# Gated DeltaNet on Trainium2: the recurrence from pair 2 on placed one slot later among the dense products

## The chip, the core and the metric

The kernel runs on one core of a Trainium2 chip. The metric is the device time of one execution in microseconds. A core has four compute engines that run their own instruction streams and meet by semaphores: TensorE (PE in the profile, with its weight loads as PEld), VectorE (DVE), ScalarE (ACT) and GpSimd (POOL). SyncE (SP) issues the DMAs of this program.

## What is computed

One inference step of a trunk of two layers over a prompt of 1024 tokens with 16 meta tokens ahead of it, and a batch of eight samples of eight tokens each. Layer 0 is a gated DeltaNet, layer 1 an RWKV-7 layer. The change concerns layer 0 alone. With `xn` the normed input, it computes (cut from the reference):

```python
proj = xn @ w_in                                     # q, k, v, z and two gates per head
qkv, new_buf = causal_conv(qkv, conv_buf, conv_w)    # 4 taps, then silu
q, k = l2norm(q) * GDN_HEAD_K ** -0.5, l2norm(k)
L = strict_lower((beta * k) @ k.T * decay)           # per chunk of 64 tokens
u, wk = solve(I + L, [beta * v, beta * k * exp(gc)])
for each chunk:                                      # the recurrence, S is [key, value]
    v_new = u - wk @ S
    o     = (q * exp(gc)) @ S + attn @ v_new
    S     = S * exp(g_last) + k_dec.T @ v_new
o = rmsnorm(o, gn_w) * silu(z)
return o @ w_out, S, new_buf
```

There are 8 key heads and 16 value heads of 128, so 8 head pairs, each one key head with its two value heads.

## The kernel before

**Tiling.** The tokens stand in three segments of 384, 384 and 336 columns (SEGS), nine token groups of 128 in all. A dense product (`product`, `halves`) is 128 output features over all tokens in split precision: per segment 24 matmuls of 128x128 by 384 or 336 columns, in two halves of 12. The 12 matmuls of a half are one *slot*. A product has six slots, two for each segment; the last two of six are the narrow ones of 336 columns.

**Order of the products.** `ORDER` (L26) lists the products by pair: k, q, and v, w (the two value heads), x, y (the gates z of the pair before); the last pair has its own gates X, Y as well. 48 products make 288 slots, numbered from −24 to 263. From pair 1 on a pair takes six products, 36 slots: pair 1's begin at slot 0, pair 2's at 36, pair 7's at 216. I call the stretch of 36 slots a period, and count its slots from 0 to 35.

**What is placed among them.** `gdn_events` (L923) fills a table of events, each with a time in slots, and a loop in `layer0` (its function `before`) emits, behind the 12 matmuls of a slot, all events whose time lies below the next slot. On TensorE and ScalarE the instructions run in just this order (`manual_schedule`). VectorE, GpSimd and SyncE are ordered by the scheduler of the framework, from the same program. Two groups of events are made for each pair j:

- `chain_events(j, G, a)` with a = first[j]: the recurrence (`gdn_recur`, 9 token groups, three steps each, a step per slot) and what goes with it: the decays and scores of attention, the token transposes (ktok), the sample states, the norm of the outputs and the gated transposes (`gdn_norm_out`, tile mog).
- `front_events(j, G, b, a, a0)` with a0 = first[j − 1]: the preparation of pair j's triangular solve while pair j − 1's recurrence runs: decays E, scores, blocks, 15 calls of the inverse (`inverse32`, L573 and L575 on VectorE), `spread` at a − 9.9 (copy invA at L743, store to DRAM as g_t and g_u, load back as T1n at L749 and TT at L756), and four merges at a − 6.5, a − 4.5, a − 3.5 and a − 1.5. The first merge issues the 72 small matmuls rY, which read T1n and E.

A token group of the recurrence reads on TensorE: S,K and S,Q (state by keys and by queries); then X,TT, where X is made on VectorE (L883); then w,ktok and w,attn, where w is scaled on ScalarE. VectorE closes the group with the new S (L905) and the output o (L916). The next group's S,K needs this S, and its PSUM tile the rA of an earlier group to be read.

The times of pair 2's `front_events` hang on first[1], those of later pairs on first[j − 1]. Not tied to first are the products, the conv taps and silus behind them (`vt`, `cvy`, `raw`), the sample keys, the weight casts (`whi`, `wlo`) and their loads (`wraw`). Weights are loaded two tiles of 256 KB at a time into two buffers, and a buffer is free when `wlo` was made from it on GpSimd. Behind slot 263 follow the rest of pair 7's recurrence, the reload of the gated outputs (`load_split`), the residual (`residual_in`) and the output projection (`gdn_out`).

Of the kernel before, what the change touches and what calls it, by code (L numbers as in the profile page):

```python
# [36 lines left out]
class Builder:  # L37
# [885 lines left out]
    def gdn_events(self, G, open_, gate, swap):  # L923

        self.events = {}
        base = [-24]
        for j in range(8):
            base.append(base[j] + 6 * min(len(ORDER[j]), 6))
        first = [9, 43] + [base[j + 1] + 6 for j in range(2, 8)]
        for u in (-23.4, -21.4, -20.4):  # L930
            self.at(u, gate)
        self.at(-13, swap)
        for j in range(8):
            self.chain_events(j, G, first[j])
            self.front_events(j, G, base[j] if j else -24, first[j], first[j - 1] if j else None, open_)
# [1618 lines left out]
```

## Time and profile before

| | us |
|---|---|
| median of 3 runs | 2171.39 |
| lowest and highest | 2170.72, 2176.32 |
| the profiled execution | 2173.21 |
| its span, first to last instruction | 2171.5 |
| mean granted TensorE clock | 0.982 |
| the stretch read below, slots 36 to 263 of layer 0's products (about) | 247 to 1015 |
| a steady period (36 slots), of which TensorE is busy | 118.80, 116.99 |

The page of the profile gives the busy time of each engine, the chain of work that ended last, and the costliest groups of instructions. A row of the timeline gives start, length, engine, line of the kernel, operation, output and inputs without buffer numbers, shape, count, and in brackets the idle time of the engine just before it with the instruction that ended it. A row of waits gives engine, waiting line, what it waited for, total us, times and the longest. In rows of windows stand the start and end, the length, busy us and count for PE, PEld, DVE, ACT and POOL, then the granted clock, the share of the DMA engines and GB/s.

### The profile page before, as it was taken

What the parts mean: (1) busy time and instruction counts of PE and PEld (TensorE: products, weight loads), DVE (VectorE), ACT (ScalarE), POOL (GpSimd) and SP (SyncE); (2) the same over time, 40 slices, a digit from 0 to 9 for tenths busy, and PEclk for the clock granted to TensorE, in tenths of its full rate; (3) what the DMA queues carried; (4) which work ended last, traced back from release to release, by engine and by line L of the source; (5) the groups of instructions that cost most, each with busy time, mean ns of one, the idle gap of its engine ahead of it and who ended that gap; (6) DMA issues with size and microseconds to landing.
All of it is one profiled execution on the core that took longest, in us unless ns stands there. A gap on an engine that the chain in (4) does not pass through costs nothing. (4 is left out here: it accounts for less than half of the span.)

```text
span 2171.5 us, 54811 instructions
## 1 busy us (share of the span) xinstructions
PE 2046.2 (94%) x20418; PEld 1905.8 (88%) x20418; DVE 1583.4 (73%) x4212; ACT 1283.1 (59%) x3750; POOL 834.9 (38%) x1136
## 2 busy tenths in 40 slices
PE   6969899999999999999999999889899999999997
PEld 5959899999999999998899999889798988888876
DVE  6968879698888979795334676757979557767755
ACT  4536565656565665656533365664747446677774
POOL 3523334334343333334231352344524254444444
PEclk9979999999999999999999999999999999999999
DMA  3424343424333333335345115655555486677754
GB/s 120 122 58 105 77 108 90 118 79 107 90 97 106 106 97 104 97 102 159 106 129 135 63 54 191 220 160 174 169 180 158 117 224 175 188 234 225 228 178 139
DMA packets 430724, 292.52 MB, mean 135 GB/s; under 512 B 147337, under 2 KB 413050, under 8 KB 430458
## 3 DMA queue, kind: packets, MB, share of 16 engines
q1 hardware_dynamic: 430458, 289.02, 46.2%
q8 instruction: 161, 2.64, 0.5%
q14 instruction: 105, 0.86, 0.1%
HBM read 197.55 MB, written 91.37 MB: 133 GB/s over the span
## 5 line engine op out<-in xcount | busy, mean ns | idle before, releaser
L91 POOL TENSOR_TENSOR wlo<-wraw,whi 128x512 fp32r<-128x512 f32 (+1 forms) x246 | 331.1, 1348 | 465.6 <-ACT whi L87 413.9
L77 PE MATMUL d<-xc,whi 128*128 128x384 f32 (+2 forms) x1006 | 279.5, 337 | 4.8 <-ACT whi L87 4.1
L526 DVE SCALAR_TENSOR_TENSOR cvy<-raw,cw,cvy 128x408 f32<-128x408 f32 (+2 forms) x288 | 199.0, 692 | 17.1 <-ACT cvy L63 15.7
L87 ACT CAST whi<-wraw 128x512 fp32r<-128x512 f32 (+1 forms) x246 | 149.8, 611 | 88.1 <-PE d L77 51.2
L77 PEld LDWEIGHTS d<-xc,whi 128*128 128x128 f32 (+1 forms) x1006 | 183.4, 189 | 7.8 <-ACT whi L87 4.8
L77 PE MATMUL d<-xc,wlo 128*128 128x384 f32 (+3 forms) x476 | 157.7, 340 | 2.7 <-POOL wlo L91 2.7
L77 PE MATMUL dz<-xc,whi 128*128 128x384 f32 (+1 forms) x480 | 153.9, 338 | 0.0
L77 PE MATMUL dv<-xc,whi 128*128 128x384 f32 (+1 forms) x480 | 152.4, 337 | 0.0
L77 PE MATMUL d<-xa,whi 128*128 128x384 f32 (+3 forms) x450 | 142.1, 340 | 4.5 <-ACT whi L87 1.7
L63 ACT ACTIVATE o<-rA,gcol 128x128 f32<-128x128 f32 x128 | 42.0, 366 | 116.9 <-DVE S L905 116.7
L573 DVE TENSOR_TENSOR invtmp<-invA,invT 72x31 f32<-72x31 f32 (+15 forms) x248 | 102.2, 412 | 3.2
L77 PE MATMUL dv<-xa,whi 128*128 128x384 f32 (+1 forms) x288 | 99.1, 344 | 0.0
L77 PE MATMUL dz<-xa,whi 128*128 128x384 f32 (+1 forms) x288 | 98.6, 342 | 0.0
L575 DVE TENSOR_TENSOR invT<-invT,invtmp 72x31 f32<-72x31 f32 (+15 forms) x248 | 95.0, 383 | 3.3
L77 PEld LDWEIGHTS d<-xc,wlo 128*128 128x128 f32 (+1 forms) x476 | 89.3, 189 | 6.8 <-POOL wlo L91 3.6
L77 PEld LDWEIGHTS dz<-xc,whi 128*128 128x128 f32 x480 | 89.4, 189 | 4.6 <-issue 4.5
L77 PEld LDWEIGHTS d<-xa,whi 128*128 128x128 f32 (+1 forms) x450 | 83.9, 189 | 8.2 <-issue 3.7
L77 PEld LDWEIGHTS dv<-xc,whi 128*128 128x128 f32 x480 | 89.2, 188 | 1.4 <-issue 1.4
L77 PE MATMUL d<-xa,wlo 128*128 128x384 f32 (+3 forms) x252 | 84.9, 337 | 1.4 <-POOL wlo L91 1.4
L77 PE MATMUL dk<-xc,whi 128*128 128x384 f32 (+1 forms) x240 | 79.3, 349 | 0.0
L77 PE MATMUL dq<-xc,whi 128*128 128x384 f32 (+1 forms) x240 | 77.0, 338 | 0.0
L1335 DVE SCALAR_TENSOR_TENSOR mixs<-xb,pcol,mixs 128x320 f32<-128x320 f32 (+2 forms) x96 | 68.6, 725 | 5.9 <-ACT mixs L63 5.6
(542 smaller groups left out, 6801.0 us busy)
## 6 DMA issues: line engine op xcount, KB each, us to landing
wraw<-in_gdn_w_in SPq DMA_DIRECT2D x96, 256.0 KB
wraw<-in_rwkv_w_rkvz SPq DMA_DIRECT2D x80, 256.0 KB
Sb<-in_state_gdn SPq DMA_DIRECT2D x64, 256.0 KB
sldcak<-cakd SPq DMA_DIRECT2D x24, 576.0 KB
wraw<-in_rwkv_w_o SPq DMA_DIRECT2D x42, 256.0 KB
E<-drow SPq DMA_DIRECT2D x24, 384.0 KB
attn<-drow SPq DMA_DIRECT2D x24, 384.0 KB
wraw<-in_gdn_w_out SPq DMA_DIRECT2D x36, 256.0 KB
```

Source lines behind the costliest of these rows:

```text
L63: return self.nc.scalar.activation(out, in_, func, bias=bias, scale=scale, **kw)
L77: self.nc.tensor.matmul(out, lhsT, rhs, start=start, stop=stop)
L87: nc.scalar.copy(hi, x)
L91: e.tensor_tensor(lo, x, hi.bitcast(F32), op=ALU.subtract)
L526: nc.vector.scalar_tensor_tensor(y[0][:, 0:wd], raw[:, k:k + wd], cw[k], y[0][:, 0:wd], op0=ALU.mult, op1=ALU.add)
L573: nc.vector.tensor_tensor(tmp, A[:, j, j + 1:32].unsqueeze(2).broadcast_to([nb, n, m]), Tv[:, j, 0:m].unsqueeze(1).broadcast_to([nb, n, m] ...
L575: nc.vector.tensor_tensor(Tv[:, j + 1:32, 0:m], Tv[:, j + 1:32, 0:m], tmp, op=ALU.subtract)
L1335: nc.vector.scalar_tensor_tensor(x[:, f:], xb[:, 8 + a + f:8 + b], mu, x[:, f:], op0=ALU.mult, op1=ALU.add)
```

## The change

One number in the table of starts: for the pairs from 2 on, the recurrence starts at the base of the next period plus 7 instead of plus 6. Pairs 0 and 1 keep their starts 9 and 43 (43 is 36 + 7).

```diff
         base = [-24]
         for j in range(8):
             base.append(base[j] + 6 * min(len(ORDER[j]), 6))
-        first = [9, 43] + [base[j + 1] + 6 for j in range(2, 8)]
+        first = [9, 43] + [base[j + 1] + 7 for j in range(2, 8)]
```

So all of `chain_events` for pairs 2 to 7 comes one slot later, the merges of pairs 2 to 7 too, and the decays, scores, inverse and spread of pairs 3 to 7. Every engine has the same instructions as before; only their order differs, and in layer 1 TensorE's order is the same.

The first place is TensorE in slot 29 and 30 of the period in which pair 5's recurrence runs (S_10372 and S_10398 are its state, dv a product of pair 6, f the transposes of values, mog the gated transposes). Before, behind the 12 matmuls of slot 29, which has 336 columns:

```order
L77 MATMUL rA_11455<-S_10372,K_8774 128x128
L77 MATMUL rA_11456<-S_10372,K_8774 128x128
L77 MATMUL rA_11455<-S_10372,Q_9575 128x128
L77 MATMUL rA_11456<-S_10372,Q_9575 128x128
L74 MATMUL f_11468<-ident_74,vt_11376 128x128 x3
L74 MATMUL mog_11478<-ident_74,o_10797 128x128
L74 MATMUL mog_11478<-ident_74,o_10909 128x128
L74 MATMUL mog_11478<-ident_74,o_11029 128x128
```

Now, in slot 30, which has 384 columns:

```order
L77 MATMUL rA_11490<-S_10398,K_8731 128x128
L77 MATMUL rA_11491<-S_10398,K_8731 128x128
L77 MATMUL rA_11490<-S_10398,Q_9552 128x128
L77 MATMUL rA_11491<-S_10398,Q_9552 128x128
L74 MATMUL mog_11507<-ident_74,o_10816 128x128
L74 MATMUL mog_11507<-ident_74,o_10929 128x128
L74 MATMUL mog_11507<-ident_74,o_11046 128x128
```

The last token group's S,K stands behind a wide slot now instead of a narrow one, and so do those of the groups that stood in slots 11, 17 and 23.

The second place is TensorE at the end of a period, slots 35 and 0, with the twelve products of a slot between them left out. Before:

```order
L74 MATMUL f_11719<-ident_74,vt_11667 128x128 x3
L77 MATMUL rY_11729<-T1n_510,E_10262 32x32 x12
L77 MATMUL rY_11730<-T1n_510,E_10354 32x32 x12
L77 MATMUL rY_11731<-T1n_510,E_10433 32x32 x12
```

and behind the next slot:

```order
L74 MATMUL mog_11807<-ident_74,o_11156 128x128
L74 MATMUL mog_11807<-ident_74,o_11318 128x128
L74 MATMUL mog_11807<-ident_74,o_11450 128x128
L74 MATMUL flast_11813<-ident_74,last_10059 108x128
```

Now the f transposes stand alone in slot 35, and behind slot 0 stand these:

```order
L77 MATMUL rY_11760<-T1n_510,E_10285 32x32 x12
L77 MATMUL rY_11761<-T1n_510,E_10372 32x32 x12
L77 MATMUL rY_11762<-T1n_510,E_10448 32x32 x12
L74 MATMUL flast_11805<-ident_74,last_10012 108x128
```

The small products rY, which read T1n, come behind slot 0 instead of slot 35, and the first three mog have gone to slot 1.

The third place is what leads to T1n of pair 6, on VectorE and on SyncE (invT_10716 and invT_10733 are the inverse, bv is made from the f transposes, ovar belongs to the norm). VectorE before:

```order
L905 SCALAR_TENSOR_TENSOR S_10372<-S_10372,eglb_136,rA_11456 128x128
L575 TENSOR_TENSOR invT_10716<-invT_10716,invtmp_11532 72x2x30
L825 TENSOR_TENSOR bv_11560<-f_11561,sk_10081 128x3x128
L573 TENSOR_TENSOR invtmp_11591<-invA_10714,invT_10716 72x31
L916 TENSOR_TENSOR o_11450<-o_11450,rA_11455 128x128
L916 TENSOR_TENSOR o_11450<-o_11450,rA_11456 128x128
L575 TENSOR_TENSOR invT_10716<-invT_10716,invtmp_11591 72x31
L526 SCALAR_TENSOR_TENSOR cvy_11567<-raw_11498,cw_404,cvy_11567 128x408
L743 COPY invA_10714<-invT_10716 72x1024
```

VectorE now:

```order
L905 SCALAR_TENSOR_TENSOR S_10398<-S_10398,eglb_136,rA_11491 128x128
L526 SCALAR_TENSOR_TENSOR cvy_11544<-raw_11469,cw_404,cvy_11544 128x408
L575 TENSOR_TENSOR invT_10733<-invT_10733,invtmp_11555 72x3x29
L916 TENSOR_TENSOR o_11485<-o_11485,rA_11490 128x128
L916 TENSOR_TENSOR o_11485<-o_11485,rA_11491 128x128
L573 TENSOR_TENSOR invtmp_11558<-invA_10731,invT_10733 72x60
L575 TENSOR_TENSOR invT_10733<-invT_10733,invtmp_11558 72x2x30
L573 TENSOR_TENSOR invtmp_11608<-invA_10731,invT_10733 72x31
L825 TENSOR_TENSOR bv_11643<-f_11644,sk_10034 128x3x128
L575 TENSOR_TENSOR invT_10733<-invT_10733,invtmp_11608 72x31
L1059 SCALAR_TENSOR_TENSOR ovar_11635<-ssq_11184,qeps_9537 128x6
L743 COPY invA_10731<-invT_10733 72x1024
```

Before, the bv ahead of the last step reads the f transposes of slot 31; now it reads those of slot 33. From the inverse's first step to the copy invA, VectorE has 140 rows instead of 136: two taps (cvy), one vt, one bv and one ovar more, one zg less. SyncE before:

```order
L920 DMA out_p_gdn<-S_10372 128x2x128
L746 DMA g_t<-invT_10716 54x1024
L745 DMA g_u<-invA_10714 72x1024
L749 DMA T1n_510<-g_t 32x18x32 x3
L756 DMA TT_13_117<-g_u 32x6x32 x4
L756 DMA TT_14_118<-g_u 32x6x32 x4
L756 DMA TT_11_115<-g_u 32x6x32 x4
L428 DMA wraw_11778<-in_gdn_w_in 128x4x128
L428 DMA wraw_11780<-in_gdn_w_in 128x4x128
```

SyncE now:

```order
L920 DMA out_p_gdn<-S_10398 128x2x128
L428 DMA wraw_11731<-in_gdn_w_in 128x4x128
L746 DMA g_t<-invT_10733 54x1024
L745 DMA g_u<-invA_10731 72x1024
L749 DMA T1n_510<-g_t 32x18x32 x3
L756 DMA TT_13_117<-g_u 32x6x32 x4
L756 DMA TT_14_118<-g_u 32x6x32 x4
L756 DMA TT_11_115<-g_u 32x6x32 x4
L428 DMA wraw_11733<-in_gdn_w_in 128x4x128
```

One of the two wraw loads stands ahead of g_t now, in all of pairs 3 to 7; for pair 2 the order of these rows is unchanged.

## Prediction

> **What bounds the kernel now.** I read the page first (parts 1 and 4), then windows over the eight pair periods of the DeltaNet layer, the waits of TensorE inside them, and the timeline at the slots that those waits name. The page:
>
> ```profile
> span 2171.5 us, 54811 instructions
> ...
> PE 2046.2 (94%) x20418; PEld 1905.8 (88%) x20418; DVE 1583.4 (73%) x4212; ACT 1283.1 (59%) x3750; POOL 834.9 (38%) x1136
> ```
>
> TensorE is busy for 94% of the span. Only the DeltaNet layer is touched, so the share has to be read there. The windows cut it by pair period (the 36 slots of six products; columns: window, length, busy us and count of PE, PEld, DVE, ACT, POOL, granted clock, DMA share, GB/s). The first row is a whole steady period, the next two lie inside it, the last is the tail behind the products:
>
> ```profile
> 734.30:853.10 118.80, 116.99 (x1027) 111.09 (x1021) 102.00 (x280) 74.17 (x246) 43.37 (x66) 1.00 0.36 100
> ...
> 831.00:842.00 11.00, 9.95 (x69) 9.47 (x68) 10.92 (x31) 5.17 (x18) 1.85 (x5) 1.00 0.32 91
> 842.00:853.10 11.10, 11.10 (x138) 10.54 (x137) 11.00 (x31) 4.73 (x14) 5.81 (x9) 1.00 0.58 146
> ...
> 1015.00:1060.00 45.00, 38.86 (x269) 35.48 (x268) 19.86 (x50) 34.61 (x153) 13.07 (x13) 1.00 0.60 182
> ```
>
> A steady period leaves TensorE 118.80 − 116.99 = 1.8 us idle, so a later recurrence can win little per period. VectorE is the second engine, and in the last 22 us of a period it is full (10.92 of 11.00, 11.00 of 11.10 us): what is put ahead of something there delays it. TensorE's waits in the five periods from pair 2's recurrence on (376.5 to 972.5; engine, line, waited for: us, times, longest):
>
> ```profile
> PE rA L77 <- DVE o L916: 4.2, 7, 0.7
> PE mog L74 <- ACT o L63: 2.4, 4, 0.6
> PE rA L77 <- DVE S L905: 1.5, 5, 0.3
> ```
>
> So 5.7 us are the recurrence's S,K products waiting for VectorE, and 2.4 us the gated output's transposes waiting for ScalarE. Where they stand in a period (start, length, instruction, idle before and its releaser):
>
> ```profile
> 832.93 0.32 PE L77 MATMUL dv<-xc,wlo 128*128 128x336 f32 x1
> 833.09 0.32 PE L77 MATMUL dv<-xc,whi 128*128 128x336 f32 x1
> 833.71 0.49 PE L77 MATMUL rA<-S,K 128*128 128x128 f32 x2 [0.31 <-DVE S L905]
> 834.95 0.49 PE L77 MATMUL rA<-S,K 128*128 128x128 f32 x2 [0.74 <-DVE o L916]
> ...
> 856.40 0.33 PE L74 MATMUL mog<-ident,o 128*128 128x128 f32 x1 [0.59 <-ACT o L63]
> ```
>
> The first two waits are in slot 29 of the period, a slot of 336 columns, which covers the chain least; the third is in slot 0 of the next. A stall costs more than its bracket: from the last dv to the S,K it waits for lie 833.71 − 833.09 = 0.62 us, where matmuls of that width follow each other 0.16 us apart (832.93 to 833.09), so 0.46 is lost for 0.31 listed. I take 1.5 times the listed idle throughout.
>
> **The change, part by part.** No instruction is added or removed; every cost is one of place.
>
> *Pair 2's T1n.* In before, the inverse's small products rY at the end of slot 71 wait for the DMA of T1n, and then the clock drops (the last rows are the same place a few pairs later, at full clock, a whole slot of dk matmuls from 853.10 to 855.31):
>
> ```profile
> 374.32 0.22 PE L77 MATMUL rY<-T1n,E 32*32 32x32 f32 x2 [0.51 <-DMA T1n<-g_t]
> 375.27 1.32 PE L77 MATMUL rY<-T1n,E 32*32 32x32 f32 x70 [0.73 <-DMA T1n<-g_t]
> ...
> 377.38 0.52 PE L77 MATMUL dk<-xa,whi 128*128 128x384 f32 x1
> 377.70 0.52 PE L77 MATMUL dk<-xa,wlo 128*128 128x384 f32 x1
> ...
> 853.10 0.45 PE L77 MATMUL dk<-xa,whi 128*128 128x384 f32 x1
> ...
> 853.74 0.34 PE L77 MATMUL dk<-xa,whi 128*128 128x384 f32 x1
> 853.91 0.34 PE L77 MATMUL dk<-xa,wlo 128*128 128x384 f32 x1
> ...
> 855.31 0.51 PE L74 MATMUL mog<-ident,o 128*128 128x128 f32 x2
> ```
>
> The window over the four microseconds behind it:
>
> ```profile
> 376.00:380.00 4.00, 4.00 (x48) 3.96 (x43) 3.84 (x12) 3.32 (x10) 0.00 (x0) 0.61 0.31 48
> ```
>
> The waits are 0.51 + 0.73 = 1.24 us. The granted clock is 0.61 in the window behind them, and dk matmuls stand 0.32 us apart where they stand 0.175 apart at full clock (853.74 to 853.91); over eleven of them that is 11 × 0.145 = 1.6 us. After the change this rY stands behind slot 72's twelve dk matmuls, 2.2 us later (855.31 − 853.10), while for pair 2 the inverse, the copy to DRAM and the load of T1n keep their place. T1n was there at 375.27, rY would come at about 376.5. Both losses go: **−2.8 us**. Ends: 0 (if the DMA slid too) and −2.8.
>
> *The mog transposes.* In pairs 2 to 6 they move from slot 0 to slot 1, together with the scaling of o ahead of them. Pair 1's recurrence already stands where the others will stand (start 43, one past 36 + 6), so its period is a mirror of what is to come; its S,K products read, in the groups of 376.5 to 972.5 (the five steady periods), of 252 to 376.5 (the mirror), and at the mirror's largest stall:
>
> ```profile
> L77 PE MATMUL rA<-S,K 128*128 128x128 f32 x160 | 29.6, 291 | 6.3 <-DVE o L916 4.2 <-DVE S L905 1.5
> ...
> L77 PE MATMUL rA<-S,K 128*128 128x128 f32 x32 | 5.6, 287 | 1.1 <-DVE o L916 1.1
> ...
> 349.78 0.49 PE L77 MATMUL rA<-S,K 128*128 128x128 f32 x2 [0.84 <-DVE o L916]
> ```
>
> The four mog waits listed above fall on four of the five boundaries behind pairs 2 to 6; pair 1's own transposes, at slots 73 and 74, do not wait. So I let 2.4 × 1.5 = 3.6 us go: **−3.6**, ends 0 (the stall moves with the work) and −3.6.
>
> *The S,K waits.* Moved by one slot, S,K no longer falls into the 336-column slots 11, 17, 23, 29 but into 12, 18, 24, 30 of 384 columns; the cover ahead of each wait grows by 12 × (0.175 − 0.155) = 0.24 us there. The mirror still stalls, at other slots (349.78 is its slot 27): 1.1 us in one period against 6.3 / 5 = 1.26. By idle alone the change is worth 5 × 0.16 = 0.8 us; if every one of these waits goes, 6.3 × 1.5 = 9.4. Pair 1's inverse runs at a closer cadence than the others', which loads VectorE differently, so the mirror is not exact. I take 0.5 per period, nearer the mirror's end: **−2.5**.
>
> *T1n of pairs 3 to 7.* Here the inverse moves as well, and it is here that the change costs. The rows of pair 6 (SyncE's issues, VectorE, TensorE):
>
> ```profile
> 843.68 0.55 DVE L825 TENSOR_TENSOR bv<-f,sk 128x384 f32<-128x384 f32 x1
> 844.15 0.17 DVE L573 TENSOR_TENSOR invtmp<-invA,invT 72x31 f32<-72x31 f32 x1
> ...
> 844.64 0.18 DVE L575 TENSOR_TENSOR invT<-invT,invtmp 72x31 f32<-72x31 f32 x1
> ...
> 844.85 0.30 SPq L746 DMA_DIRECT2D g_t<-invT  x1
> ...
> 846.88 0.55 PE L74 MATMUL f<-ident,vt 128*128 128x128 f32 x3
> 847.18 0.40 PE L77 MATMUL dv<-xa,whi 128*128 128x336 f32 x1
> ...
> 851.84 1.33 PE L77 MATMUL rY<-T1n,E 32*32 32x32 f32 x72
> ```
>
> And of pair 2 the issue of the same transfer:
>
> ```profile
> 368.52 0.34 SPq L746 DMA_DIRECT2D g_t<-invT  x1
> ```
>
> Today the inverse's last step runs at 844.64, g_t is issued at 844.85, and rY at 851.84 does not wait: 6.99 us were enough. Pair 2 tells what the way takes: issue at 368.52, released at 375.27, 6.75 us. The margin is thin, 0.24 us by that row. After the change rY comes one slot later: from the start of slot 34 (847.18) it is 851.84 − 847.18 = 4.66, plus a slot of twelve dk matmuls, 855.31 − 853.10 = 2.21, so 6.87 us. The new start of the way has two parts. First, the order on VectorE puts a bv that needs the f transposes of slot 33 (846.88 above, done at slot 34's start) ahead of the inverse's last step: bv 0.47 (843.68 to 844.15), the step 0.18 and 0.1 to the issue put g_t at slot 34 + 0.7. T1n lands at 0.7 + 6.75 = 7.45 against 6.87: a wait of 0.6. Secondly, two taps, one vt and one bv more and one zg less now stand between the first step of the inverse and its copy, about 1.9 us of conv work on a VectorE that is full there, and SyncE now issues a 256 KB wraw load ahead of g_t; at 146 GB/s for a DMA share of 0.58 (row 842.00:853.10) the sixteen engines move 252 GB/s, so that load takes 1.0 us of them. If both come in full the wait is 0.6 + 1.9 + 1.0 = 3.5 us; if T1n lands somewhat faster than pair 2's, nothing waits. Much of the 1.9 is done while VectorE would stand for f anyway, so I take 1.3 us, nearer the low end: 5 × 1.3 = **+6.5**, ends 0 and +17.5. Behind the waiting rY are TensorE's flast and all products of the next pair; nothing covers it.
>
> *The clock behind these waits.* At slot 71 a wait of 1.24 us beside 72 small matmuls was enough for the slow stretch that cost 1.6 us; rY without a wait (851.84) was followed by full speed. For waits of 1.3 us I put it at two of the five boundaries: 2 × 1.6 = **+3.2**, ends 0 and +8. The Trainium skill, TensorE: Matmul & The Clock Gate, section HAM oscillation, states as its rule that gaps of TensorE above about 3.4 us are to be avoided. By that rule, waits of 1.3 us cost no clock, and the sum would be 3.2 less. The trace does not agree: the waits at slot 71 are 0.51 and 0.73 us, and the clock fell.
>
> *The tail.* One more slot of pair 7's recurrence falls behind the last product, among the work whose waits of TensorE from 1009 to 1060 read:
>
> ```profile
> PE f L74 <- ACT xb L1166: 2.3, 3, 1.4
> PE f L74 <- DMA stage<-in_x_prompt: 1.4, 2, 0.7
> PE rA L77 <- DVE X L883: 1.3, 1, 1.3
> ```
>
> TensorE is idle there for 6.1 us of 45, mostly for other things than the chain, and the output projection that follows does not need pair 7 at first. The moved step is a few matmuls of 0.3 us. Ends: −1.3 (the wait for X goes) and one uncovered slot, +2.2; I take **+0.5**.
>
> Sum: −2.8 − 3.6 − 2.5 + 6.5 + 3.2 + 0.5 = +1.3. The profiled execution took 2173.2 us (span 2171.5 and 1.7 around it), 1.8 above the median of 2171.39; 2173.2 + 1.3 − 1.8 = 2172.7, so I forecast **2172.7 us**, no change that could be told: with runs that lie 5.6 us apart, less than 0.3% (6.5 us) cannot be told from none.
>
> **The rivals.**
>
> *T1n arrives in time.* The way from g_t takes 6.0 us or so instead of 6.75 where fewer transfers run beside it, and VectorE does the extra taps while it waits for f. Then the gains stand alone: −8.9 + 0.5, 2163 us. For it: five steady periods of before show no rY wait at all with a margin of 0.24 by pair 2's price, so their price must be at or below 6.99. Against it: bv and wraw ahead of g_t.
>
> *Late at every boundary (slower).* The place is rY at slot 0 of pairs 3 to 7, the mechanism the load of T1n behind a later inverse. It decides from the point where g_t is issued more than 6.87 − 6.75 = 0.1 us after slot 34's start; every us beyond is a us of TensorE, and from about 1.2 us on the slow clock comes with it. With a wait in the middle of the upper half, 2.3 us, and 1.6 of clock: 5 × 3.9 = 19.5 − 8.9 + 0.5 = +11, 2182.5 us. For it: VectorE full from 831 on. Against it: the inverse is ordered early and only the conv work is new ahead of it.
>
> *Waits cost only themselves.* The clock stays up behind waits of 1.3 us, as it does behind the 0.74 at 834.95: 2172.7 − 3.2 = 2169.5. Against it: slot 71. By the rule of the Trainium skill (TensorE: Matmul & The Clock Gate, section HAM oscillation) the clock would stay up as well.
>
> **How the numbers follow.** The forecast has 0.45 (own range 2166 to 2179: stalls that move along with the work on one side, longer waits on the other), T1n in time 0.24, late everywhere 0.20, waits without clock 0.11. Faster by over 0.3% (below 2164.9) is most of the second case and a little of the first: 0.26. Slower by over 0.3% (above 2177.9) is nearly all of the third and a little of the first: 0.25. The rest, 0.49, is no change. The range goes from 2161, a little below T1n in time, to 2183, just above late everywhere; stalls that all vanish (9.4 instead of 2.5) and waits of 3.5 us lie outside.
>
> **What would show it.** Right: no rY wait at 374 and no clock below 0.9 from 376 to 380; mog without a wait at the period's start; S,K waits of about 1 us a period at slots 24 to 30; rY at the end of slot 0 of pairs 3 to 7 with a wait of 0.6 to 2 us on T1n, and g_t issued 0.7 to 2 us after slot 34's start. Wrong: rY without a wait there (the first rival, 2163), rY waits above 2 us with half clock behind each (the second), mog or S,K waits as large as before at their new slots, or a tail from 1015 to 1060 that grows by more than 2 us.

## The result, and the profile after

The changed kernel takes 2189.53 us (median of 10 runs, 2185.39 to 2192.77), the kernel before 2172.35 us in the same comparison (10 runs). The ratio is 1.0069, 95% interval 1.0053 to 1.0085: slower by 0.69%, about 15 us. The forecast was 2172.7 us and no change, with a range to 2183; the time lies outside it. Of the rivals, "late at every boundary" (2182.5) had the sign, and was 7 us short.

The page of the changed kernel:

```profile
span 2187.4 us, 54775 instructions
...
PE 2054.9 (94%) x20418; PEld 1915.2 (88%) x20418; DVE 1576.8 (72%) x4212; ACT 1286.3 (59%) x3750; POOL 847.3 (39%) x1136
```

The same instructions take 15.9 us longer from first to last (2187.4 against 2171.5). Where, is told by the starts of the same slots in the two profiles:

| start of | before | after | difference |
|---|---|---|---|
| slot 36 | 247.2 | 247.5 | +0.3 |
| slot 66 | 357.1 | 358.5 | +1.3 |
| slot 71 | 371.4 | 372.7 | +1.3 |
| slot 73 | 380.3 | 378.5 | −1.8 |
| slot 107 | 492.6 | 491.4 | −1.1 |
| slot 143 | 611.7 | 612.4 | +0.7 |
| slot 179 | 730.7 | 733.6 | +2.9 |
| slot 215 | 849.5 | 853.5 | +4.0 |
| slot 251 | 968.4 | 977.0 | +8.6 |
| slot 258 | 994.4 | 1005.4 | +11.0 |
| second half of the output projection | 1148.7 | 1162.6 | +13.9 |
| last instruction | 2171.5 | 2187.4 | +15.9 |

The slots are chosen so that TensorE has the same work behind it in both kernels. Slots 72, 108 and so on up to 252 would mislead: the 72 matmuls rY stand ahead of their start before and behind it now, which alone shifts the start by about 1.3 us. The 1.3 us at slot 66 are scatter, since TensorE's order is the same up to there. In the other runs below whose order is the same up to there, slot 66 starts up to 1.3 us earlier than in the kernel before, or at the same time; so a difference of 1 or 2 us between two profiles says little.

Pair 2's boundary gains 3.1 us (slot 71 to 73), slots 73 to 251 lose 10.4, the boundary into pair 7's period 2.4 (slot 251 to 258), the way from there to the second half of the output projection 2.9, and the rest, mostly layer 1, 2.0. In the windows (columns as before) the period that answers to the one shown of before is 119.90 us long with TensorE busy for 116.61, so 3.3 us idle instead of 1.8:

```profile
736.30:856.20 119.90, 116.61 (x1024) 111.14 (x1022) 99.66 (x281) 74.59 (x245) 45.90 (x68) 1.00 0.35 98
...
845.20:856.20 11.00, 10.67 (x75) 10.37 (x73) 10.89 (x31) 7.06 (x23) 5.55 (x6) 1.00 0.43 133
```

VectorE is as full at the end of the period as it was (10.89 of 11.00). TensorE's waits in the five periods:

```profile
PE rA L77 <- DVE o L916: 4.8, 7, 0.9
PE rA L77 <- DVE S L905: 4.2, 5, 0.9
PE rY L77 <- DMA T1n<-g_t: 3.5, 7, 0.8
PE f L74 <- DVE vt L532: 2.1, 5, 0.6
PE mog L74 <- DVE zg L1077: 1.5, 3, 0.7
PE fss L74 <- DVE hist L490: 0.5, 1, 0.5
```

They sum to 16.6 us, against 8.1 in the three rows of before and 0.4 of f; the last boundary's rY, 1.48 us, stands just behind this stretch, so rY waits 5.0 us in all. The wait of mog for ScalarE's o is gone, as forecast; rY waits, as forecast; but the recurrence waits more than before (9.0 against 5.7), and f, mog and fss wait for VectorE, of which before had only that 0.4 of f. The places, pair 2's rY first, then one boundary and the slots ahead of it:

```profile
377.14 1.33 PE L77 MATMUL rY<-T1n,E 32*32 32x32 f32 x72
...
830.38 0.49 PE L77 MATMUL rA<-S,K 128*128 128x128 f32 x2 [0.86 <-DVE S L905]
831.72 0.49 PE L77 MATMUL rA<-S,K 128*128 128x128 f32 x2 [0.85 <-DVE o L916]
...
851.19 0.40 PE L77 MATMUL dv<-xa,whi 128*128 128x336 f32 x1
...
853.56 0.31 SPq L746 DMA_DIRECT2D g_t<-invT  x1
...
858.99 0.22 PE L77 MATMUL rY<-T1n,E 32*32 32x32 f32 x2 [0.48 <-DMA T1n<-g_t]
860.03 1.32 PE L77 MATMUL rY<-T1n,E 32*32 32x32 f32 x70 [0.82 <-DMA T1n<-g_t]
```

and the window behind that rY:

```profile
861.90:865.30 3.40, 3.40 (x13) 3.31 (x12) 3.23 (x9) 0.94 (x5) 0.00 (x0) 0.50 0.34 54
```

Pair 2's rY does not wait any more. Pair 6's g_t is issued 2.37 us after slot 34's start (851.19), rY waits 0.48 + 0.82, and the clock is halved for 3.4 us. S,K waits 0.86 + 0.85 in slot 27, a slot of 384 columns, and not for the last token group in slot 30 but for the one ahead of it. The other four periods have the same pair of waits in slot 27.

Why S is late there was not in the prediction. Four engines have to be read side by side. SyncE, GpSimd, VectorE of the changed kernel, ahead of that S,K:

```profile
818.17 0.38 SPq L428 DMA_DIRECT2D wraw<-in_gdn_w_in  x1
818.65 0.45 SPq L649 DMA_DIRECT2D attn<-drow  x1
...
822.86 1.38 POOL L653 TENSOR_SCALAR_AFFINE_SELECT attn<-attn 128x768 f32<-128x768 f32 x1 [4.41 <-DMA attn<-drow]
...
825.09 1.32 POOL L103 TENSOR_TENSOR ors<-ovar,cvals 128x6 f32<-128x6 f32 x1
...
826.44 0.17 DVE L111 TENSOR_TENSOR on_t<-ors 128x6 f32<-128x6 f32 x1 [1.48 <-POOL ors L103]
...
829.57 0.50 DVE L532 SCALAR_TENSOR_TENSOR Q<-raw,cvy 128x336 f32<-128x336 f32 x1
829.99 0.34 DVE L905 SCALAR_TENSOR_TENSOR S<-S,eglb,rA 128x128 f32<-128x128 f32 x1
```

GpSimd's mask of the next pair's attn waits 4.41 us for its load (3.8 to 4.5 us in the five periods), which SyncE issued behind a wraw. Behind the mask stands ors, the seed of the output norm, and VectorE, whose next row reads it, stands idle for 1.48 us while its taps, its inverse and then S queue up; S starts at 829.99, 2.8 us into slot 27, and lets S,K go at 830.38. In the kernel before, the same two rows of GpSimd and this S read:

```profile
814.64 1.05 POOL L653 TENSOR_SCALAR_AFFINE_SELECT attn<-attn 128x768 f32<-128x768 f32 x1
...
816.96 2.38 POOL L103 TENSOR_TENSOR ors<-ovar,cvals 128x6 f32<-128x6 f32 x1 [0.96 <-DVE ovar L1059]
...
822.61 0.59 DVE L905 SCALAR_TENSOR_TENSOR S<-S,eglb,rA 128x128 f32<-128x128 f32 x2
```

There the load had landed, and ors waited for its own input, not for the mask; S was done before its S,K came up in slot 26, which did not wait. That wraw is what makes the load late is read from the order of issues; no run moves it. So two theories stood: A, the loss is T1n's lateness at rY; B, it is the recurrence's own, by GpSimd's order.

### The profile page after: what moved, and what is told of

It is laid out like the page before. It is cut to its first block, busy times and chain, and to the rows that moved or that the text cites. A ratio compares the mean times of both kernels' runs of the same rounds, so it can differ in the third digit from the quotient of the medians.

```text
span 2187.4 us, 54775 instructions
## 1 busy us (share of the span) xinstructions
PE 2054.9 (94%) x20418; PEld 1915.2 (88%) x20418; DVE 1576.8 (72%) x4212; ACT 1286.3 (59%) x3750; POOL 847.3 (39%) x1136
## 5 line engine op out<-in xcount | busy, mean ns | idle before, releaser
L91 POOL TENSOR_TENSOR wlo<-wraw,whi 128x512 fp32r<-128x512 f32 (+1 forms) x246 | 342.2, 1393 | 429.8 <-ACT whi L87 392.9
L526 DVE SCALAR_TENSOR_TENSOR cvy<-raw,cw,cvy 128x408 f32<-128x408 f32 (+2 forms) x288 | 199.5, 693 | 12.9 <-ACT cvy L63 10.7
L573 DVE TENSOR_TENSOR invtmp<-invA,invT 72x31 f32<-72x31 f32 (+15 forms) x248 | 97.3, 392 | 2.8
L63 ACT ACTIVATE w<-rA,nbp 128x128 f32<-128x128 f32 x144 | 46.7, 373 | 46.1 <-PE rA L77 46.0
```

Source lines behind the costliest of these rows:

```text
L63: return self.nc.scalar.activation(out, in_, func, bias=bias, scale=scale, **kw)
L91: e.tensor_tensor(lo, x, hi.bitcast(F32), op=ALU.subtract)
L526: nc.vector.scalar_tensor_tensor(y[0][:, 0:wd], raw[:, k:k + wd], cw[k], y[0][:, 0:wd], op0=ALU.mult, op1=ALU.add)
L573: nc.vector.tensor_tensor(tmp, A[:, j, j + 1:32].unsqueeze(2).broadcast_to([nb, n, m]), Tv[:, j, 0:m].unsqueeze(1).broadcast_to([nb, n, m] ...
```

## The experiments

Ratios are to the kernel before in the same comparison. *Front* is short for decays, scores, inverse, spread and merges of pairs 3 to 7 with the merges of pair 2, *recurrence* for all of `chain_events`.

| run | recurrence | front | ratio | 95% interval |
|---|---|---|---|---|
| the change | +1 | +1 | 1.0069 | 1.0053 to 1.0085 |
| e1 | +1 | old | 1.0015 | 1.0001 to 1.0029 |
| e2 | old | +1 | 1.0154 | 1.0132 to 1.0176 |
| e3 | +1, ors first | +1 | 1.0029 | 1.0017 to 1.0041 |
| e4 | +1, ors first | old | 1.0027 | 1.0010 to 1.0044 |
| e5 | +1 | old, merges +1 | 0.9996 | 0.9982 to 1.0010 |
| e6 | +1 for pair 2 alone | merges of pair 2 | 1.0000 | 0.9987 to 1.0013 |
| e7 | old | inverse and spread +1 | 1.0146 | 1.0128 to 1.0163 |
| e8 | +1 for pair 7 alone | merges and spread of pair 7 | 1.0018 | 1.0005 to 1.0030 |
| e9 | +1 for 2 to 6 | old, merges +1 for 2 to 6 | 1.0003 | 0.9988 to 1.0018 |
| e10 | old, ors first | old | 0.9997 | 0.9984 to 1.0010 |
| e11 | +1 for 2 to 6 | +1, but pair 7's merges and spread old | 1.0055 | 1.0036 to 1.0074 |

**e1, the front put back.**

```diff
-            self.front_events(j, G, base[j] if j else -24, first[j], first[j - 1] if j else None, open_)
+            f = [p - 1 * (i > 1) for i, p in enumerate(first)]
+            self.front_events(j, G, base[j] if j else -24, f[j], f[j - 1] if j else None, open_)
```

> The recurrence stays one slot later as in the change, but decays, scores, inverse, spread and merges of pairs 3 to 7 (and the merges of pair 2) go back to their old slots. Theory A (the time is lost by T1n, which reaches rY late, and by the slow clock behind that wait): the 5.0 us of rY waits go, with them about 4 us of slow clock in slot 1 of a period, so about 10 of the 17 us: near 2180 us. Theory B (the time is lost in the recurrence itself, whose state S is late on VectorE in slot 26 to 27, because the norm's seed ors stands on GpSimd behind the mask of attn, which waits for its load): S,K waits stay near 9 us, rY waits go, the time stays above 2185. If both hold, about 2180 with S,K waits still at 9 us.

Most of the loss goes (1.0015). TensorE's waits in the five periods of e1:

```profile
PE rA L77 <- DVE o L916: 6.0, 11, 0.8
PE rY L77 <- DMA T1n<-g_t: 5.4, 6, 1.1
```

Neither theory had this. rY, back at its old slot, still waits 5.4 us, and S,K does not wait for S any more (S comes 1.8 us into slot 27 instead of 2.8), though on GpSimd ors still stands behind a mask that waits 3.1 to 4.0 us. So that order alone does not make S late; the late front has to come with it. As for rY, g_t is issued 0.7 us ahead of slot 34 here, against 2.3 in the kernel before, although the front has its old slots; why is not shown. What is left of the S,K waits are mostly two a period, 0.29 us in slot 24 and 0.84 in slot 27, the stalls of the mirror in the kernel before (0.24 and 0.84). So the mirror was right for the recurrence alone, but it holds no gain: S,K waits 6.0 us here and 5.7 in the kernel before.

**e2, only the front late.** The kernel before, with

```diff
-            self.front_events(j, G, base[j] if j else -24, first[j], first[j - 1] if j else None, open_)
+            f = [p + 1 * (i > 1) for i, p in enumerate(first)]
+            self.front_events(j, G, base[j] if j else -24, f[j], f[j - 1] if j else None, open_)
```

> The recurrence stays at its old slot, and only decays, scores, inverse, spread and merges of pairs 3 to 7 (and the merges of pair 2) come one slot later. Theory A: rY of pairs 3 to 7 waits for T1n by about 1 us each, some with slow clock behind: 2172 + 5 to 11 = 2177 to 2183 us. Theory B alone: no more than 2174, since the masks and the recurrence stand as before; S,K waits stay near 6 us.

Slower by 1.54%, 33 us, three times what theory A allows, and twice what the change costs. rY does not wait; instead:

```profile
PE mog L74 <- ACT o L63: 8.9, 8, 1.8
PE f L74 <- DVE vt L532: 5.9, 6, 1.2
PE rA L77 <- DVE o L916: 5.6, 11, 0.8
PE rA L77 <- DVE S L905: 5.0, 10, 0.6
```

All but ScalarE's o wait for VectorE directly. Each of the five boundaries also has a stretch of 3.4 or 6.8 us at half clock, which makes up to 13.7 of the 33 us. The front's place is what costs, and moving the recurrence along with it, as the change does, takes half of that back.

**e3, ors ahead of the mask.**

```diff
-        self.nc.gpsimd.tensor_tensor(y, x, half.broadcast_to(sh), op=ALU.pow)
+        r = self.nc.gpsimd.tensor_tensor(y, x, half.broadcast_to(sh), op=ALU.pow)
+        if tag == "on":
+            self.ors.append(r.ins)
...
-        nc.gpsimd.affine_select(E6, E6, pattern=[[0, 6], [1, 128]], compare_op=ALU.is_ge, fill=NEG, base=0, channel_multiplier=-1)
+        with self.tc.issue_after(self.ors[-2 if s == 0 else -1]) if tag == "attn" and self.ors else ExitStack():
+            nc.gpsimd.affine_select(E6, E6, pattern=[[0, 6], [1, 128]], compare_op=ALU.is_ge, fill=NEG, base=0, channel_multiplier=-1)
...
-        self.slot = self.anchor = None
+        self.slot, self.anchor, self.ors = None, None, []
```

> The change, with one order on GpSimd put back: each seed ors of the norm is issued ahead of the next mask of attn instead of behind it. Theory B: VectorE's waits for ors fall from 24 us to about 13, S is no longer late in slot 27, the S,K waits fall from 9 us to 4 to 6, and the slow clock in slot 28 goes: 2189.5 − 6 to 10 = 2180 to 2184 us. Theory A, or VectorE being full there anyway: S,K waits stay at 9 us and the time at 2187 to 2190.

The ratio falls from 1.0069 to 1.0029, by 0.4% or 9 us, at the upper end of theory B. The place on GpSimd and VectorE, then the waits of TensorE in the five periods:

```profile
820.66 1.92 POOL L103 TENSOR_TENSOR ors<-ovar,cvals 128x6 f32<-128x6 f32 x1 [4.25 <-DVE ovar L1062]
822.54 0.87 POOL L656 TENSOR_SCALAR_AFFINE_SELECT attn<-attn 128x768 f32<-128x768 f32 x1
822.61 0.81 DVE L113 TENSOR_TENSOR on_t<-ors 128x6 f32<-128x6 f32 x1 [0.31 <-POOL ors L103]
...
826.83 0.33 DVE L908 SCALAR_TENSOR_TENSOR S<-S,eglb,rA 128x128 f32<-128x128 f32 x1
```

```profile
PE rY L77 <- DMA T1n<-g_t: 5.0, 8, 0.8
PE rA L77 <- DVE o L919: 4.8, 7, 0.9
PE fss L74 <- DVE hist L492: 1.0, 2, 0.6
PE mog L74 <- DVE zg L1080: 0.9, 3, 0.4
```

VectorE stands 0.31 us instead of 1.48, S comes 1.8 us into slot 27 instead of 2.8 in each of the five periods, and the wait of S,K for S, 4.2 us in the change, is gone altogether; the wait for o is the same 4.8. Both slow stretches behind slot 27's S,K are gone as well. VectorE's waits for ors fall only from 23.0 to 17.3 us, not to the 13 expected. rY waits a little more than without the edit (5.0 against 3.5, for the same four boundaries). So B is shown: in the change, beside the late front, GpSimd's order costs about 9 us.

**e4, both put back.** The edits of e1 and e3 together.

> The recurrence one slot later, with both put back: decays, scores, inverse, spread and merges at their old slots, and each seed ors ahead of the next mask of attn. If A and B are the two causes and add up, rY waits are zero, S,K waits 4 to 6 us, and the time is 2168 to 2174 us, that of the kernel before or a little less (pair 2's wait at slot 71 may come back, 2.8 us). If a third cause holds, the time stays above 2178.

1.0027, not below e1's 1.0015, and rY waits 5.4 us, as in e1. The two do not add up. With the front at its old slots S is in time anyway, so ors ahead of the mask has nothing to save. As I read it, both edits relieve one thing, VectorE's queue from slot 24 to the end of the period.

**e5, a late reader with an early inverse.** e1, with the merges one slot later again:

```diff
-            at(a + u, lambda n=n: g().merges[n]())
+            at(a + (j > 1) + u, lambda n=n: g().merges[n]())
```

> As e1 (recurrence one slot later, decays, scores, inverse and spread at their old slots), but the merges, with rY ahead, stay one slot later as in the change. So T1n has the old start and the new, later reader. If T1n's lateness at rY is all that is left of the loss in e1, the rY waits of 5.4 us go, S,K waits stay at the 6 us of e1, mog does not wait, and the time is 5 to 10 us below e1: 2165 to 2172 against a before of 2172, that is ratio 0.997 to 1.000. If rY was waiting beside other work that is late as well (f and vt, TT), the waits move there and the ratio stays at e1's 1.0015.

TensorE's waits in the periods of e5 up to slot 252:

```profile
PE rA L77 <- DVE o L916: 6.9, 14, 0.8
PE f L74 <- DVE vt L532: 2.1, 3, 1.2
PE rY L77 <- DMA T1n<-g_t: 1.3, 2, 0.7
PE rA L77 <- DVE S L905: 0.9, 2, 0.5
PE mog L74 <- DVE zg L1078: 0.9, 1, 0.9
```

With the last boundary rY waits 1.5 us instead of 5.4, but the waits move: S,K waits 7.8 us instead of 6.0, and f and mog wait 3.0. From slot 71 to 73, pair 2's boundary, the profile gains 3.1 us on the kernel before; from there to slot 251 nothing more (2.9 in all). So of the three gains that the prediction summed the first is there, and the mog and S,K gains are not, even when the inverse isn't moved. The timed ratio is 0.9996, and its interval holds both a gain of 3 us and none.

**e6, pair 2 alone.**

```diff
-        first = [9, 43] + [base[j + 1] + 6 for j in range(2, 8)]
+        first = [9, 43, base[3] + 7] + [base[j + 1] + 6 for j in range(3, 8)]
```

Pair 3's front keeps its slots (a0 is taken as before).

> The kernel before, with only pair 2's recurrence and merges one slot later; decays, scores, inverse and spread of pair 3 stay. This measures the first gain of the prediction by itself: rY's wait at slot 71 and the slow clock behind it go, 2.8 us, ratio 0.9987. A rival is that pair 2's own period (slots 72 to 108) loses as much to S,K, f or T1n of pair 3: ratio 1.000.

Slot 73 starts 3.2 us earlier (377.1 against 380.3), where slot 71 started at the same time, close to the 2.8 of the prediction; at slots 107 and 251 1.9 and 1.8 of it are left. Behind slot 107 rY of pair 3 waits 0.9 us, and mog waits 0.9 for VectorE. The timed ratio is 1.0000, within whose interval both the 0.9987 of the forecast and nothing lie.

**e7, the inverse alone.** The kernel before with

```diff
-                inv, per, kk, ss, rd = [k + 9.3 + n for n in range(15)], 2, (b + 11.8, qb + 4.2), b + 13.2, (qb + 6.4, qb + 9.9)
-                sp = a - 9.9
+                inv, per, kk, ss, rd = [k + 10.3 + n for n in range(15)], 2, (b + 11.8, qb + 4.2), b + 13.2, (qb + 6.4, qb + 9.9)
+                sp = a - 8.9
```

> The kernel before, with only the 15 calls of the inverse and the spread of pairs 3 to 7 one slot later; decays, scores, merges and the recurrence stay. If the inverse on VectorE is what made e2 slow by 33 us, this is slow by at least 15 us too, with rY waits on T1n of 1 to 3 us a period, since its merges are not moved, and f, mog and S,K waiting for VectorE. If it was the later merges, decays or scores, the time stays within 5 us of before but for rY waits.

1.0146: the inverse and its spread by themselves cost as much as e2. f and S,K wait for VectorE as long as in e2, but the rest is another wait: rY for T1n, 16.4 us, where e2 had mog for ScalarE. Here rY keeps its slot and shows how late T1n comes; the waits, and one of the boundaries:

```profile
PE rY L77 <- DMA T1n<-g_t: 16.4, 9, 3.4
PE rA L77 <- DVE o L916: 6.1, 13, 0.8
PE f L74 <- DVE vt L532: 5.7, 5, 1.2
PE rA L77 <- DVE S L905: 5.1, 10, 0.6
```

```profile
874.98 0.30 SPq L746 DMA_DIRECT2D g_t<-invT  x1
...
880.76 0.28 PE L77 MATMUL rY<-T1n,E 32*32 32x32 f32 x2 [3.02 <-DMA T1n<-g_t]
881.30 2.13 PE L77 MATMUL rY<-T1n,E 32*32 32x32 f32 x70 [0.26 <-DMA T1n<-g_t]
```

One slot later at its start is more than that at its end. Counted from the start of the period of slot 180, the inverse's first step and the copy behind its last are at

```
             first step   copy invA
before          59.7        111.0
the change      63.3        117.2
e1              55.3        110.1
e3              64.6        117.2
e7              62.6        118.6
```

In e7 the start slips by 2.9 us, the end by 7.6. Part of that is TensorE's own lateness: slot 34 starts 114.9 us into the period in e7 and in the change, 112.9 before. Against that slot the copy comes 5.6 us later in e7 and 4.2 in the change. Windows of the kernel before ahead of and behind slot 20 of that period show why (VectorE's busy time is the third pair of numbers):

```profile
790.30:801.50 11.20, 11.20 (x80) 11.20 (x79) 7.05 (x24) 7.54 (x29) 4.00 (x4) 1.00 0.19 49
...
815.00:831.00 16.00, 16.00 (x155) 15.10 (x155) 15.32 (x41) 9.90 (x35) 6.55 (x11) 1.00 0.23 67
```

VectorE is a third free where the inverse begins and full where it goes on and ends. As I read it, what it leaves undone in the free part it does among the conv work of the slots behind, which then comes first in more places. In the change the recurrence and rY move along, so the same lateness (6.2 us at the copy) meets readers that are a slot later.

**e8, the tail.** The kernel before, with

```diff
-        first = [9, 43] + [base[j + 1] + 6 for j in range(2, 8)]
+        first = [9, 43] + [base[j + 1] + 6 + (j > 6) for j in range(2, 8)]
```

> The kernel before, with only pair 7's recurrence, merges and spread one slot later (its inverse stays). It measures the tail: the change ended 2.9 us later from slot 258 to the output projection. If that is one slot of the recurrence behind the last product, the time is 2 to 4 us above before, ratio 1.001 to 1.002; by the prediction's term 0.5 us, ratio 1.000.

1.0018, 3.9 us, with an interval from 1.1 to 6.5. In the profile, slot 258 moves by 2.7 us against slot 251. TensorE at the boundary of slot 252 of e8, and the window behind it:

```profile
972.48 0.33 PE L74 MATMUL mog<-ident,o 128*128 128x128 f32 x1 [1.06 <-ACT o L63]
973.40 0.33 PE L74 MATMUL mog<-ident,o 128*128 128x128 f32 x1 [0.59 <-ACT o L63]
```

```profile
975.50:978.90 3.40, 3.40 (x13) 3.30 (x12) 2.94 (x8) 0.10 (x1) 0.00 (x0) 0.50 0.09 28
```

So part of the loss is not behind the last product but at the boundary into pair 7's own period, where waits of 1.65 us, against 0.8 before, bring 3.4 us of half clock with them. From slot 258 to the second half of the output projection e8 loses 3.6 us more, with another 3.4 us of half clock at 1030. e6, whose pair 7 is not moved, has such a stretch there too, so how much of this belongs to pair 7 stays open.

**e9, e5 without pair 7.** e5 for pairs 2 to 6, pair 7 as before:

```diff
-        first = [9, 43] + [base[j + 1] + 7 for j in range(2, 8)]
+        first = [9, 43] + [base[j + 1] + 6 + (j < 7) for j in range(2, 8)]
...
+            f = [p - (1 < i < 7) for i, p in enumerate(first)]
...
+            at(a + (1 < j < 7) + u, lambda n=n: g().merges[n]())
```

> As e5 (recurrence and merges one slot later, decays, scores, inverse and spread at their old slots), but for pairs 2 to 6 alone; pair 7 stays wholly as before. e5 was 5.0 us ahead of before at slot 252 and gave 4 back behind it; e8 shows that pair 7's shift costs 4 us by itself. If the two are independent, this ends 4 to 5 us below before: ratio 0.9975 to 0.9985, about 2168 us against 2172. If the gain to slot 252 is taken back by something else behind it (the reload of stage tiles, layer 1), the ratio stays at 1.000.

1.0003: the 4 us were not to be had. In its profile the second half of the output projection starts 2.5 us earlier than in the kernel before, but 1.3 of these are there at slot 71 already, where both orders are still the same. The 1.2 us that remain lie within the interval of the timed ratio. Within what these comparisons can tell, 0.15%, no version here beats the kernel before.

**e10, the control for e3**: e3's edit on the kernel before.

> Control for e3: the kernel before, with each seed ors of the norm issued ahead of the next mask of attn on GpSimd. There the attn load mostly lands before its mask, and S is not late in slot 27, so by theory B the order should hardly matter: ratio 0.999 to 1.001. If it gains as much as e3 did on the change (0.4%), e3 does not speak of the change.

0.9997. The order on GpSimd costs nothing in the kernel before, so e3's 0.4% belongs to the change. It costs nothing there although the load is late at one of two places: the second mask of each period, in slot 33, waits 4.0 to 4.2 us for its load with an ors behind it. As I read it, what counts is how much VectorE has to do behind that ors.

**e11, the change without pair 7's recurrence.** Only the line of `first` of e9.

> The change for pairs 2 to 6 alone; pair 7's recurrence and merges keep their old slot (its decays, scores and inverse follow pair 6's recurrence and stay late). If the tail's 4 us come from pair 7's shift, this ends about 4 us below the change: ratio to before 1.004 to 1.006. If pair 7's inverse being late matters more than its recurrence, rY of pair 7 at slot 251 waits for T1n by 2 to 3 us, and the ratio stays at 1.007 or above.

1.0055, 3 us below the change, but the intervals overlap. rY of pair 7 waits 3.0 us for T1n at 981.0, as the second reading expected, so the two effects work against each other here, and the tail is better read from e8.

## Why the prediction was wrong, step by step

**Pair 2's T1n: right.** Forecast −2.8; slot 71 to 73 gained 3.1 us in the change and as much in e6. No wait and no slow clock at that boundary.

**The mog transposes: half right.** The wait for ScalarE's o went, 2.4 us as listed. But mog, fss and f now wait for VectorE, 1.5 + 0.5 + 2.1 = 4.1 us listed where before had 0.4 of f. The forecast took −3.6 and gave no price to the next thing on that engine. That waits move with the work was named as this term's zero end.

**The S,K waits: wrong, and the main error.** Forecast −2.5, from the mirror; measured, 9.0 us listed instead of 5.7, and behind them twice a slow clock (at 711.7 and 954.1). e1 shows that the mirror's stalls come back when the front keeps its place, and that even then nothing is gained (6.0 us). The prediction remarked that pair 1's inverse stands differently, and used the mirror nonetheless. (In the mirror's period it is pair 2's inverse that runs, also at the closer cadence.) What was missed is a chain over three queues: wraw ahead of attn on SyncE, attn's mask ahead of ors on GpSimd, ors ahead of S on VectorE, with the late front beside it. It stood in the orders of GpSimd and SyncE, which were read for g_t alone. e3 puts 9 us on it: with the −2.5 of the forecast, that is 11.5 of the 14 us between forecast and measurement.

**T1n of pairs 3 to 7: right in place, and in size partly by luck.** Forecast 1.3 us at each of five boundaries; the waits were 1.10, 0.75, 0.38, 1.30 and 1.48, 5.0 in all against 6.5. The way to it was not as drawn: g_t came 1.7 to 2.6 us after slot 34's start, where 0.7 to 2 were named. The way from g_t was shorter than pair 2's 6.75 us (5.9 to 6.7), and rY itself was later too, since f ahead of it waits for VectorE (0.3 to 0.6 us). The three errors largely cancel. Bv, conv work and wraw were named as what stands ahead of g_t; that the whole inverse slips, by 4.2 us at its copy against slot 34, was not. With rY at its old slot a late inverse costs 32 us (e7), with the recurrence moved along half of that or less.

**The clock: too low.** Two slow stretches were forecast, 3.2 us; three of the five boundaries have one (behind the waits of 1.10, 1.30 and 1.48, not behind 0.75 and 0.38), and two more stand behind the S,K waits of slot 27. Five stretches of 3.41 us at half clock are up to 8.5 us, the end of the range that was given. Between slots 73 and 258 the listed waits of TensorE grow from 8.8 to 18.2 us; with the clock that is 17.9 us, where 12.9 were lost, so the rest of TensorE's time got 5 us shorter, which I have not traced.

**The tail: wrong size.** Forecast +0.5, with +2.2 as the far end; e8 gives 3.9, with an interval that still holds 2.2. The step looked for the cost behind the last product alone; in e8's profile 2.7 us of it come up between slots 251 and 258.

**The rest.** 2.0 us of the 15.9 between the two profiles appear behind the start of the second half of the output projection, mostly in layer 1, where TensorE's order is the same. From the second half of the output projection to the end the thirteen profiles of this case take 1022 to 1031 us, and the kernel before 1022.8, so these 2.0 us cannot be told from scatter.

The error has a common form. Each term was priced at one wait, with VectorE's fullness as a remark on one of them (T1n). Since VectorE is full from slot 20 on, what comes later there delays, as I read it, all that follows: S, f's vt, hist, zg and the inverse at once. The third rival, that waits cost only themselves, is refuted by the five slow stretches.

## What to carry to other kernels

When a group of work is moved on an engine that is full for part of the period, count from where the engine is still free to where it is full: work that leaves the free part comes out at the end later than it was moved, here 7.6 us for one slot of about 3, of which 2.0 are TensorE's own lateness. Read the new order of every queue the moved work touches, the idle ones too: GpSimd was busy for 38% of the span, and its order cost 9 us because one of its rows waits for a load and another has a full VectorE behind it; with the front at its old slots (e1, e4) the same order cost nothing that could be told. When two profiles are compared by the start of the same piece of work, the same work must stand ahead of it in both. A stretch that already has the new order is a good mirror only when its producers stand as they will stand.

## What the runs showed of the hardware

The granted clock of TensorE halves for stretches of 3.41 us, or two or three of them, behind or during waits, most of them around the 32x32 products. It happened behind waits of 1.10, 1.30 and 1.48 us in the change and of 1.27 and 1.59 in e3, but not behind 1.21, 0.97 and 1.69 in e3; at each boundary of e7, with waits of 3.2 to 3.4 us, and there for 6.83 us or more. So the length of a wait alone does not decide it. In each trace the stretches start on a grid of 3.413 us: in the change those at 500.1, 711.7, 861.9, 954.1 and 984.8 lie 62, 44, 27 and 9 steps apart. What counts may be how much idle time falls within one step: e3's 1.69 us are split by the grid into 1.13 and 0.56, while the change's 1.48 lie within one step. This is read from the traces; no run tests it, and e3's 1.21 us lie within one step too. The Trainium skill, TensorE: Matmul & The Clock Gate, section HAM oscillation, puts the limit for gaps at about 3.4 us; the longest single gap of e7, 3.38 us, agrees; its other gaps, 2.7 to 3.0 us, and the boundaries of the change and of e3 do not.
